# Up stage of a hybrid attention block: which k tiles take their long passes before their short ones

## The chip, the cores and the metric

The kernel runs on one core of one Trainium2 chip. The metric is the device time of one execution in microseconds (us). Three executions of the kernel before gave 1472.08, 1472.37 and 1472.39 us; the median is 1472.37 us.

## The reference, cut to what matters

One block with 256 rows of width 2048 is computed in float32: three kinds of attention with gates, an output projection, and then a feed-forward part. The change lies in the feed-forward part's first product, which the kernel calls `u`:

```python
h2 = rms_norm(x, g_ffn[l])
u = causal_depthwise_conv(h2 @ w_up[l], conv_w[l], conv_b[l])   # [256, 2048] @ [2048, 11264]
u_gate, u_val = jnp.split(u, 2, axis=-1)
x = x + (jax.nn.silu(u_gate) * u_val) @ w_down[l]
```

## The kernel before, in words

**Stages.** Memory keys and values, the input projections (tiles named `f`, `s`, `g`, `xg`), the branch products (`b`), the output projection (`xo`, `yo`), the up stage (`u`) and the down stage (`xd`, `yd`) follow each other on TensorE. The up stage is the loop at L1138.

**Two parts of every number.** A float32 value is kept as a rounded part `hi` and a remainder `lo`, and a product is made of three of the four partial products: hi by hi, hi by lo, lo by hi. For the up stage the 256 rows of the normalised input stand transposed in `hT`, one [128, 512] slice for each of 16 k tiles (a k tile is 128 of the 2048 contracted columns): its first 256 columns are the `hi` part of all rows, the other 256 the `lo` part.

**Rounds and half rounds.** The loop takes 11 values of `f0` (0, 4, ... 40; each is four blocks of 128 feed-forward columns) and for each of them two values of `s` (0 for the gate half of `w_up`, 1 for the value half). I call one pair (f0, s) a half round; there are 22, and each has 16 k tiles and four PSUM banks, one for each block of 128 columns.

**One k tile.** It has eight matmuls. A *long pass* (L1155) has a [128, 128] block of weights `hi` as the stationary operand and streams all 512 columns of `hT`. A *short pass* (L1157) has the block of weights `lo` and streams only the first 256 columns. There is one of each for each of the four banks. The list `UP_ORDER` (L39) gives them in turn: long, short, long, short and so on, bank by bank. A k tile for which `grouped` is true (L1151) is sorted by kind instead: four long passes, then four short ones. In the kernel before, the first four k tiles of each half round are grouped while f0 is 0 or 4, and only the first k tile of each half round after that.

**What feeds it.** `piece` (L136) loads two k tiles of weights (512 KB) on the SyncE queue, ScalarE rounds them to `hi` (L142) and VectorE forms `lo` (L143); `hi` and `lo` have four buffers each.

**What stands among the passes.** After each pair of k tiles `tick` lets the deferred work go on: the convolution of the half round before (`conv`, L1114), sums of weights for the down stage (`weight_sums`, L244), and in the first half round the last 16 transposes of the input (L196) after the fourth k tile. Two transposes (L1049), which spread the row scale, stand between the first and the second half round. The helper functions `in_order` and `pin` fix some of the order; the rest is put in place by a scheduler.

Of the kernel before, what the change touches and what calls it, by code (L numbers as in the profile page):

```python
# [42 lines left out]
def hybrid_block(  # L43
# [38 lines left out]
    def bank(name):  # L82
        return pp.tile([P, 512], F32, tag="bank", name=name)
# [14 lines left out]
    def later(gen):  # L98
        waiting.append(gen)
# [3 lines left out]
    def tick(beside=True):  # L103
        if beside:
            for g in background:
                next(g, None)
        while waiting and len(active) < WINDOW:
            active.append([waiting.popleft(), 0])
        for a in list(active):
            if a[1] > 0:  # L110
                a[1] -= 1
                continue
            try:
                a[1] = next(a[0]) or 0
            except StopIteration:
                active.remove(a)
# [19 lines left out]
    def piece(src, a, n, name):  # L136
        raw = wp.tile([P, PIECE], F32, tag="raw", name=f"raw_{name}")
        hi = wp.tile([P, PIECE], F32R, tag="hi", bufs=SBUFS, name=f"hi_{name}")
        lo = wp.tile([P, PIECE], F32R, tag="lo", bufs=SBUFS, name=f"lo_{name}")
        m = a * n  # L140
        pin(nc.sync.dma_start(raw[:, :m].rearrange("p (a n) -> p a n", a=a), src))
        pin(nc.scalar.copy(hi[:, :m], raw[:, :m]))  # L142
        pin(nc.vector.tensor_tensor(lo[:, :m], raw[:, :m], hi[:, :m].bitcast(F32), ALU.subtract))  # L143
        return (
            hi[:, :m].rearrange("p (a n) -> p a n", a=a),
            lo[:, :m].rearrange("p (a n) -> p a n", a=a),
        )
# [525 lines left out]
    for k in range(KT):  # L673
# [18 lines left out]
        for _ in range(0 if k < 3 else 1 if k < 8 else 3):  # L692
            if squares:
                j, t = squares.popleft()
# [419 lines left out]
    def conv(ps, f, s):  # L1114
        if not pads:
            padded()
        ct = s * FT + f
        cr = cp.tile([P, S], F32, tag="cr", bufs=2, name=f"cr_{f}_{s}")
        nc.scalar.copy(cr, ps[:, S:])
        u = pads[f % 2]  # L1120
        nc.vector.tensor_tensor(cr, cr, ps[:, :S], ALU.add)
        nc.vector.tensor_tensor(u[:, 2:], cr, rbc, ALU.mult)  # L1122
        y = cp.tile([P, S], F32, tag="y", bufs=6, name=f"y_{f}_{s}")
        tap = lambda j: taps[:, j, ct : ct + 1]
        nc.scalar.activation(y, u[:, 2:], AF.Identity, scale=tap(2), bias=tap(3))  # L1125
        nc.vector.scalar_tensor_tensor(y, u[:, 1 : S + 1], tap(1), y, ALU.mult, ALU.add)
        nc.vector.scalar_tensor_tensor(y, u[:, 0:S], tap(0), y, ALU.mult, ALU.add)
        if s == 0:
            nc.scalar.activation(y, y, AF.Silu)
            ys[f] = y  # L1130
        else:
            g = ys.pop(f)
            nc.vector.tensor_tensor(g, g, y, ALU.mult)
            split_to(a_pair(f // 2)[:, f % 2], g)
        return
        yield

    for f0 in range(0, FT, 4):  # L1138
        if f0 == FA:
            assert not halves  # L1140
            for g in background:
                deque(g, 0)
            background.clear()
        for s in range(2):
            ps = [bank(f"u{f0 + i}_{s}") for i in range(4)]
            c0 = s * D_FF + f0 * P
            for k in range(0, KT, 2):
                hi, lo = piece(upv[:, k : k + 2, c0 : c0 + 512], 2, 512, f"u{f0}_{s}_{k}")
                for j in range(2):
                    first, last = k + j == 0, k + j == KT - 1  # L1150
                    grouped = k + j < (4 if f0 < 8 else 1)  # L1151
                    for i, part in sorted(UP_ORDER, key=lambda ip: ip[1]) if grouped else UP_ORDER:
                        c = slice(i * P, (i + 1) * P)
                        if part == 0:
                            nc.tensor.matmul(ps[i], lhsT=hi[:, j, c], rhs=hT(k + j), start=first, stop=False)  # L1155
                        else:
                            nc.tensor.matmul(  # L1157
                                ps[i][:, :S], lhsT=lo[:, j, c], rhs=hT(k + j)[:, :S], start=False, stop=last
                            )
                tick()  # L1160
            for i in range(4):
                later(conv(ps[i], f0 + i, s))
# [90 lines left out]
```

## Time and profile before

| what | value |
|---|---|
| median of three executions | 1472.37 us |
| the profiled execution, its own time | 1472.16 us |
| its span in the profile | 1470.4 us |
| TensorE clock granted | 1.0 |
| first long pass of the up stage starts | 746.85 us |
| first matmul of the down stage starts | 1242.02 us |
| passes in the up stage | 1408 long, 1408 short |

The profiled execution lasted 1.8 us longer than its span, which counts from the first to the last instruction. Times in the views are counted from the span's start. A matmul's row gives its start and a duration that includes the time in the array's pipeline; consecutive matmuls overlap, so what a matmul costs is the step from its start to the start of the next.

### The profile page before, as it was taken

The numbers are of one execution on the slowest core, as the hardware profiler recorded it, in microseconds if no ns is written. First come the engines' busy times: TensorE is split into PE (matmuls) and PEld (weight loads), VectorE is DVE, ScalarE is ACT, GpSimd is POOL, SyncE is SP. The second block draws the span as 40 slices with busy tenths as digits, with TensorE's granted clock in tenths as the row PEclk, the third lists the DMA queues.
The fourth block names the chain that finished last, engine by engine and source line by source line (L and its number), as shares of the span: only waits on it lengthen the run. The fifth ranks groups of instructions, "written<-read, shape, count | busy, mean of one in ns | idle before, by whom it ended". The sixth has DMA issues, their size and how long they took to land.

```text
span 1470.4 us, 20665 instructions
## 1 busy us (share of the span) xinstructions
PE 1465.3 (100%) x7337; PEld 1239.1 (84%) x7337; DVE 1194.0 (81%) x1818; ACT 840.0 (57%) x1194; POOL 20.4 (1%) x46
## 2 busy tenths in 40 slices
PE   9999999999999999999999999999999999999998
PEld 7888888888888888888888888888888888888887
DVE  5777676777588899897888889888888877997877
ACT  6755454464364555546666556556556555674664
POOL 0000000021000000000000000000000000000000
PEclk9999999999999999999999999999999999999999
DMA  9686787687868576778768888889888866798796
GB/s 311 199 276 191 219 285 214 185 268 222 248 196 279 160 236 202 274 249 278 248 208 275 278 279 289 274 277 287 287 280 283 260 188 199 248 317 274 262 319 225
DMA packets 205527, 369.42 MB, mean 251 GB/s; under 512 B 13531, under 2 KB 82031, under 8 KB 205167
## 3 DMA queue, kind: packets, MB, share of 16 engines
q1 hardware_dynamic: 204094, 365.99, 78.0%
q10 hardware_dynamic: 1328, 2.11, 0.4%
q8 instruction: 57, 0.93, 0.2%
q14 instruction: 48, 0.39, 0.1%
HBM read 335.54 MB, written 32.51 MB: 250 GB/s over the span
## 4 chain that ended last, share of the span: by engine, by line
PE 99%; DVE 0%; ACT 0%; POOL 0%; issue 0%; POOLq 0%; DVEq 0%
PE u L1155 22%; PE u L1157 11%; PE xd L289 4%; PE xd L288 4%; PE xd L287 4%; PE xg L289 3%; PE xg L288 3%; PE xg L287 3%; PE f L289 2%; PE f L287 2%; PE f L288 2%; PE s L287 2%; PE s L289 2%; PE s L288 2%; PE b L289 2%; PE g L287 2%
## 5 line engine op out<-in xcount | busy, mean ns | idle before, releaser
L1155 PE MATMUL u<-hT,hi_u 128*128 128x512 f32 x1232 | 422.1, 395 | 0.0
L1157 PE MATMUL u<-hT,lo_u 128*128 128x256 f32 x1232 | 328.9, 280 | 0.0
L1155 PEld LDWEIGHTS u<-hT,hi_u 128*128 128x128 f32 x1232 | 228.8, 188 | 51.6
L143 DVE TENSOR_TENSOR lo_u<-raw_u,hi_u 128x1024 fp32r<-128x1024 f32 x176 | 214.9, 1221 | 68.9 <-ACT hi_u L142 67.9
L142 ACT CAST hi_u<-raw_u 128x1024 fp32r<-128x1024 f32 x176 | 184.8, 1050 | 142.9 <-PE u L1155 129.8
L1157 PEld LDWEIGHTS u<-hT,lo_u 128*128 128x128 f32 x1232 | 227.9, 189 | 2.9
L282 DVE TENSOR_TENSOR lo_d<-raw_d,hi_d 128x1024 fp32r<-128x1024 f32 x88 | 106.7, 1222 | 20.7 <-ACT hi_d L281 18.0
L281 ACT CAST hi_d<-raw_d 128x1024 fp32r<-128x1024 f32 x88 | 92.1, 1054 | 48.0 <-PE xd L288 23.0
L281 ACT CAST hi_g<-raw_g 128x1024 fp32r<-128x1024 f32 (+1 forms) x64 | 61.7, 972 | 37.2 <-PE xg L288 14.2
L282 DVE TENSOR_TENSOR lo_g<-raw_g,hi_g 128x1024 fp32r<-128x1024 f32 (+1 forms) x64 | 70.7, 1117 | 4.1 <-ACT hi_g L281 4.1
L142 ACT CAST hi_f<-raw_f 128x1024 fp32r<-128x1024 f32 (+1 forms) x40 | 38.6, 968 | 52.2 <-PE f L288 47.3
L143 DVE TENSOR_TENSOR lo_f<-raw_f,hi_f 128x1024 fp32r<-128x1024 f32 (+1 forms) x40 | 44.7, 1119 | 28.0 <-ACT hi_f L142 26.1
L288 PE MATMUL xd<-hi_d,aT 128*128 128x512 f32 x170 | 66.2, 389 | 0.0
L287 PE MATMUL xd<-hi_d,aT 128*128 128x512 f32 x170 | 66.2, 389 | 0.0
L289 PE MATMUL xd<-lo_d,aT 128*128 128x512 f32 x170 | 66.1, 389 | 0.0
L143 DVE TENSOR_TENSOR lo_s<-raw_s,hi_s 128x1024 fp32r<-128x1024 f32 (+1 forms) x40 | 44.7, 1117 | 25.3 <-ACT hi_s L142 25.0
L142 ACT CAST hi_s<-raw_s 128x1024 fp32r<-128x1024 f32 (+1 forms) x40 | 38.4, 961 | 43.9 <-PE s L288 27.1
L1155 PE MATMUL u<-hT_rest,hi_u 128*128 128x512 f32 x176 | 62.7, 396 | 0.0
L143 DVE TENSOR_TENSOR lo_g<-raw_g,hi_g 128x1024 fp32r<-128x1024 f32 x32 | 39.3, 1233 | 22.6 <-ACT hi_g L142 22.2
L1125 ACT ACTIVATE y<-u,taps 128x256 f32<-128x256 f32 x88 | 49.2, 595 | 14.5 <-DVE u L1122 14.5
L142 ACT CAST hi_b<-raw_b 128x1024 fp32r<-128x1024 f32 x32 | 33.6, 1052 | 41.6 <-PE b L288 15.3
L142 ACT CAST hi_g<-raw_g 128x1024 fp32r<-128x1024 f32 x32 | 33.6, 1051 | 37.6 <-PE g L288 35.3
(481 smaller groups left out, 3532.1 us busy)
## 6 DMA issues: line engine op xcount, KB each, us to landing
raw_u<-in_w_up_dram SPq DMA_DIRECT2D x176, 512.0 KB, 4.9
raw_g<-in_w_in_dram SPq DMA_DIRECT2D x96, 512.0 KB, 4.5
raw_d<-in_w_down_dram SPq DMA_DIRECT2D x66, 512.0 KB, 5.4
pre_d<-in_w_down_dram SPq DMA_DIRECT2D x88, 256.0 KB, 4.3
kept_d<-pre_d SPq DMA_DIRECT2D x44, 512.0 KB, 6.1
raw_f<-in_w_in_dram SPq DMA_DIRECT2D x32, 512.0 KB, 4.6
raw_s<-in_w_in_dram SPq DMA_DIRECT2D x32, 512.0 KB, 4.2
raw_o<-in_w_out_dram SPq DMA_DIRECT2D x25, 512.0 KB, 5.1
```

What stands on the lines that cost most here:

```text
L142: pin(nc.scalar.copy(hi[:, :m], raw[:, :m]))
L143: pin(nc.vector.tensor_tensor(lo[:, :m], raw[:, :m], hi[:, :m].bitcast(F32), ALU.subtract))
L281: nc.scalar.copy(hi[:, :n], src)
L282: nc.vector.tensor_tensor(lo[:, :n], src, hi[:, :n].bitcast(F32), ALU.subtract)
L287: fix(nc.tensor.matmul(o, lhsT=ah, rhs=w[0], start=first, stop=False))
L288: fix(nc.tensor.matmul(o, lhsT=al, rhs=w[0], start=False, stop=False))
L289: fix(nc.tensor.matmul(o, lhsT=ah, rhs=w[1], start=False, stop=last))
L1125: nc.scalar.activation(y, u[:, 2:], AF.Identity, scale=tap(2), bias=tap(3))
L1155: nc.tensor.matmul(ps[i], lhsT=hi[:, j, c], rhs=hT(k + j), start=first, stop=False)
L1157: nc.tensor.matmul(ps[i][:, :S], lhsT=lo[:, j, c], rhs=hT(k + j)[:, :S], start=False, stop=last)
```

## The change

One line is changed. After it, exactly one k tile of the whole stage is grouped: f0 = 4, s = 0, k tile 0, the first of the third half round. The other 33 k tiles that were grouped take long and short passes in turn.

```diff
                 for j in range(2):
                     first, last = k + j == 0, k + j == KT - 1
-                    grouped = k + j < (4 if f0 < 8 else 1)
+                    grouped = (f0, s, k + j) == (4, 0, 0)
                     for i, part in sorted(UP_ORDER, key=lambda ip: ip[1]) if grouped else UP_ORDER:
```

No pass is added or removed. The order of the built program moves on TensorE in these k tiles alone. On VectorE one `lo` (second half round, first pair of k tiles) goes ahead of the copy that feeds the two transposes of L1049. On the SyncE queue one load of the second half round's weights (k tiles 8 and 9) goes ahead of one load for the down stage. ScalarE and GpSimd keep their order.

## Prediction

> **What bounds the kernel now.** I read the page first: its span, the busy shares, the chain that ended last, and the groups of the two lines that change.
>
> ```profile
> span 1470.4 us, 20665 instructions
> ...
> PE 99%; DVE 0%; ACT 0%; POOL 0%; issue 0%; POOLq 0%; DVEq 0%
> ...
> L1155 PE MATMUL u<-hT,hi_u 128*128 128x512 f32 x1232 | 422.1, 395 | 0.0
> L1157 PE MATMUL u<-hT,lo_u 128*128 128x256 f32 x1232 | 328.9, 280 | 0.0
> ...
> L142 ACT CAST hi_u<-raw_u 128x1024 fp32r<-128x1024 f32 x176 | 184.8, 1050 | 142.9 <-PE u L1155 129.8
> ```
>
> TensorE is the chain (99%), and the passes have no idle time ahead of them (0.0 in the last column). ScalarE waits for TensorE to free weight buffers (129.8 us), not the other way round. So only the steps between matmuls can change the time. Next I asked for the stretches between the first long passes of half rounds: the first seven, then the last two.
>
> ```profile
> 746.85:770.97 24.12, 24.12 (x148) 21.36 (x146) 19.19 (x32) 17.18 (x31) 0.00 (x0) 1.00 0.68 203
> 770.97:793.62 22.65, 22.65 (x132) 19.68 (x130) 18.76 (x32) 14.21 (x21) 0.00 (x0) 1.00 0.85 267
> 793.62:816.19 22.57, 22.57 (x131) 19.62 (x129) 20.66 (x39) 13.13 (x20) 0.00 (x0) 1.00 0.86 269
> 816.19:838.76 22.57, 22.57 (x130) 19.62 (x129) 18.46 (x31) 13.18 (x20) 0.00 (x0) 1.00 0.89 291
> 838.76:860.97 22.21, 22.21 (x131) 19.57 (x130) 20.52 (x39) 13.20 (x20) 0.00 (x0) 1.00 0.86 267
> 860.97:883.57 22.60, 22.60 (x131) 19.60 (x129) 18.48 (x31) 13.10 (x20) 0.00 (x0) 1.00 0.90 294
> 883.57:905.77 22.20, 22.20 (x130) 19.56 (x129) 20.50 (x39) 13.23 (x20) 0.00 (x0) 1.00 0.85 271
> ...
> 1197.22:1219.42 22.20, 22.20 (x131) 19.56 (x129) 18.14 (x33) 13.11 (x20) 0.00 (x0) 1.00 0.62 187
> 1219.42:1242.02 22.60, 22.60 (x130) 19.60 (x129) 15.57 (x25) 13.07 (x20) 0.00 (x0) 1.00 0.61 186
> ```
>
> The first numbers are the length, then TensorE's busy time. From the fifth half round on, equal work takes 22.20 us and 22.60 us in turn, at a granted clock of 1.00. The last two rows have far less DMA (187 GB/s against 271 and 294) and the same two lengths, so transfers are not the reason. The timeline of TensorE shows it pass by pass; first from the sixth half round (22.60), then from the seventh (22.20).
>
> ```profile
> 870.14 0.40 PE L1155 MATMUL u<-hT,hi_u 128*128 128x512 f32 x1
> 870.38 0.28 PE L1157 MATMUL u<-hT,lo_u 128*128 128x256 f32 x1
> 870.50 0.40 PE L1155 MATMUL u<-hT,hi_u 128*128 128x512 f32 x1
> 870.73 0.28 PE L1157 MATMUL u<-hT,lo_u 128*128 128x256 f32 x1
> 870.85 0.40 PE L1155 MATMUL u<-hT,hi_u 128*128 128x512 f32 x1
> 871.08 0.28 PE L1157 MATMUL u<-hT,lo_u 128*128 128x256 f32 x1
> 871.20 0.40 PE L1155 MATMUL u<-hT,hi_u 128*128 128x512 f32 x1
> ```
>
> ```profile
> 889.83 0.39 PE L1155 MATMUL u<-hT,hi_u 128*128 128x512 f32 x1
> 890.05 0.28 PE L1157 MATMUL u<-hT,lo_u 128*128 128x256 f32 x1
> 890.17 0.39 PE L1155 MATMUL u<-hT,hi_u 128*128 128x512 f32 x1
> ...
> 890.52 0.39 PE L1155 MATMUL u<-hT,hi_u 128*128 128x512 f32 x1
> ```
>
> Long and short passes in turn run in one of two gaits. In the dragging gait three pairs take 1.06 us (870.14 to 871.20) and the long steps differ: 0.24, 0.23, 0.23. That is 0.3533 us a pair, 1.413 us for a k tile of four pairs. In the quick gait two pairs take 0.69 us (889.83 to 890.52). Fifteen alternating tiles of a 22.20 half round, less the grouped one worked out next, give it better: (22.20 - 1.40) / 15 = 1.387 us. A gait, once there, holds for all 15 alternating tiles. The grouped tile's own cost is in the chain that ended last, at the sixth and the seventh half round:
>
> ```profile
> 861.13 0.92 PE u L1155 x4
> 862.05 0.48 PE u L1157 x4
> 862.53 0.23 PE u L1155
> ...
> 883.73 0.93 PE u L1155 x4
> 884.66 0.47 PE u L1157 x4
> 885.13 0.23 PE u L1155
> ```
>
> 862.53 - 861.13 = 1.40 us, and 885.13 - 883.73 = 1.40 us: between the gaits. What matters is what it leaves behind. **One grouped tile turns the gait over**: quick before 861.13 and dragging after it, dragging before 883.73 and quick after it, and so on to the end. **Four in a row leave it as it was**: the second, third and fourth half rounds drag (22.65, 22.57, 22.57), though the third and fourth begin with four grouped tiles each. Check: 4 x 1.40 + 12 x 1.413 = 22.56.
>
> The TensorE page of the Trainium skill (TensorE: Matmul & The Clock Gate, "Back-to-back issue gap") gives a gap that depends on the streamed columns alone. By it the order would be worth nothing, and the time would stay 1472.4. The 22.20 and 22.60 of one workload speak against it.
>
> **The change part by part.** The profiled execution (1472.16) stands 0.2 below the median (1472.37); I sum on the first and add 0.2.
>
> The question is the gait ahead of the one tile left. The two transposes of L1049 come just before the second half round:
>
> ```profile
> 752.43 1.91 PE L196 MATMUL hT<-ident,xres_again 128*128 128x128 f32 x16
> 754.10 0.47 PE L1155 MATMUL u<-hT,hi_u 128*128 128x512 f32 x1
> 754.41 0.28 PE L1157 MATMUL u<-hT,lo_u 128*128 128x256 f32 x1
> 754.53 0.40 PE L1155 MATMUL u<-hT,hi_u 128*128 128x512 f32 x1
> ...
> 770.83 0.38 PE L1049 MATMUL rp<-ident,rb 128*128 128x128 f32 x2
> 770.97 1.18 PE L1155 MATMUL u<-hT,hi_u 128*128 128x512 f32 x4
> ```
>
> From 754.10 to 770.83 there are twelve alternating tiles: 16.73 / 12 = 1.394, quick but for the start. Then come two transposes and four grouped tiles, and the gait drags. If four grouped tiles change nothing, the two transposes did it, and without the grouped tiles the second half round drags from its start. Then the tile at (4, 0, 0) turns the gait to quick, and nothing later turns it back. I choose this. The sum:
>
> - First half round: four grouped tiles (752.43 - 746.85 = 5.58) become alternating, in a gait not seen there: 5.55 (quick) to 5.65 (dragging); I take the middle, +0.02, and keep both ends. The 16 transposes stay where they are.
> - Second: 12 tiles drag already; the first four, 22.65 - 12 x 1.413 = 5.69, become 5.65: -0.04.
> - Third: 1.40 + 15 x 1.387 = 22.20 for 22.57: -0.37.
> - Fourth: 16 x 1.387 = 22.19 for 22.57: -0.38.
> - Nine half rounds of 22.20 (s = 0) become 22.19, by unrounded steps 0.02 less: -0.16 together.
> - Nine of 22.60 (s = 1) become 22.19: 9 x -0.415 = -3.73.
>
> Together -4.66, so 1467.5, and **1467.7 us** against the median (-0.32%).
>
> Cover. A short pass is wanted earlier where grouping is gone: the first 0.23 after the start instead of 0.90. The nearest `lo` is the stage's first, and its row in VectorE's timeline is
>
> ```profile
> 742.17 1.22 DVE L143 TENSOR_TENSOR lo_u<-raw_u,hi_u 128x1024 fp32r<-128x1024 f32 x1
> ...
> 764.11 0.29 DVE L1045 COPY rb<-scales 128x256 f32<-128x256 f32 x1
> ```
>
> It ends at 743.39, 3.5 us ahead of the stage, so this costs nothing; without that cover it would be at most the 0.67 by which the use moves. The copy `rb`, now behind a `lo` of 1.22, ends near 765.6 instead of 764.40, 5 us before the transposes at 770.83 that read it. On SyncE's queue one load for the down stage comes one 512 KB load later; the down stage starts 470 us after that. Loads that start up to 2% sooner meet a DMA share of 0.85 to 0.90 with ScalarE waiting for TensorE, so nothing is late next.
>
> **The rivals.**
>
> *The transposes leave the quick gait, and the one tile turns it to dragging (slower).* For it: 16 transposes at 752.43 are followed by alternating passes directly, and these are quick from the second pair on; the two of L1049 may do the same, and the second half round's first grouped tile, which starts out of transposes, may not turn the gait as later ones do. Against it: four grouped tiles then led from quick to dragging, which four do nowhere else. It decides at the third half round's first tile. Price: second half round 22.65 to 22.20, -0.45; third 1.40 + 15 x 1.413 = 22.60, +0.03; fourth 22.61, +0.04; nine of 22.20 become 22.61, +3.67; nine of 22.60, +0.09. Sum +3.4: 1475.8 (+0.23%).
>
> *Quick everywhere.* The transposes leave the quick gait and the one tile does not turn it, because this quick gait grew out of transposes and not out of a grouped tile. The forecast less the second half round's 0.41: 1467.3.
>
> *No difference.* The gaits in the long stretches without a grouped tile fall into each other, or mix: between the two ends, 1472.4 if half of it drags as now. Against it: neither gait decays within 15 tiles anywhere.
>
> **How the numbers follow.** The forecast gets 0.52, quick everywhere 0.08, the slower rival 0.33, no difference 0.07. About 0.2% (2.9 us) is what a measurement of this kernel can tell from no change, so the slower rival (+3.4) lies just outside, and I count a small part of it as no change: faster 0.60, same 0.10, slower 0.30. The forecast's own range is 1467.0 to 1468.4 (the unknown first four tiles, the spread of runs of 0.3). It and quick everywhere hold only 0.60, so the range must reach to the slower rival: 1466.8 to 1476.2.
>
> **What would show it.** Right: the second half round takes 22.6, the third 22.2, and all later ones 22.19; the grouped tile at about 793.6 costs 1.40; the down stage starts 4.7 us sooner. Wrong: a second half round of 22.2 and 22.6 from the third on (first rival); 22.19 from the second on (quick everywhere). If the gait changes in the middle of a half round, or TensorE has idle time ahead of a pass in this stage, the whole reading is wrong.

## The result, and the profile after

| | before | after |
|---|---|---|
| median | 1472.35 us (11 runs) | 1475.68 us (11 runs) |
| profiled execution, its own time and span | 1472.16, 1470.4 us | 1475.68, 1474.0 us |
| up stage, first long pass to first matmul of the down stage | 746.85 to 1242.02: 495.17 us | 746.43 to 1245.53: 499.10 us |

The kernel after is slower: 1.0023 times the time before, 95% interval [1.0014, 1.0032]. The forecast was 1467.7 us and faster. All of the loss is in the up stage, which grew by 3.93 us; in the profiled execution the stage began 0.42 us earlier, which is why the span grew by no more than 3.6.

The profile page's group lines of the kernel after hold the first hint. They are the same two groups, long and short passes, that the prediction quotes of before: busy time, mean ns of one, idle time ahead.

```profile
L1155 PE MATMUL u<-hT,hi_u 128*128 128x512 f32 x1232 | 435.9, 399 | 0.0
L1157 PE MATMUL u<-hT,lo_u 128*128 128x256 f32 x1232 | 345.4, 281 | 0.0
```

There is no idle time ahead of a pass in either kernel, and the number of passes is the same. But a long pass lasts 399 ns in the mean and not 395, a short one 281 and not 280. The half rounds of the kernel after, the second to the fourth and the last (length first, then TensorE's busy time, granted clock as the third number from the end):

```profile
770.60:793.29 22.69, 22.69 (x131) 19.68 (x130) 18.90 (x32) 14.28 (x21) 0.00 (x0) 1.00 0.89 273
793.29:815.88 22.59, 22.59 (x130) 19.60 (x129) 20.68 (x39) 13.21 (x20) 0.00 (x0) 1.00 0.88 268
815.88:838.49 22.61, 22.61 (x130) 19.60 (x129) 18.46 (x31) 13.08 (x20) 0.00 (x0) 1.00 0.89 291
...
1222.92:1245.53 22.61, 22.61 (x131) 19.60 (x129) 15.55 (x25) 13.08 (x20) 0.00 (x0) 1.00 0.59 184
```

The second half round drags, as the forecast said. The third begins with the grouped tile, and it drags too, as does every one after it. The quick half rounds of before (22.20) are gone: nine of them lose 0.41 us each, 3.7 us; the other 13 add the remaining 0.2 or so. So the second half round came out as I had read the transposes, and **the grouped tile did not turn the gait**.

Its surroundings say why it might not. First TensorE's timeline of the kernel before, at a tile that turned the drag into the quick gait (883.57); then that of the kernel after, at its one tile (793.29).

```profile
882.86 0.40 PE L1155 MATMUL u<-hT_rest,hi_u 128*128 128x512 f32 x1
883.10 0.28 PE L1157 MATMUL u<-hT_rest,lo_u 128*128 128x256 f32 x1
883.22 0.40 PE L1155 MATMUL u<-hT_rest,hi_u 128*128 128x512 f32 x1
...
883.57 1.09 PE L1155 MATMUL u<-hT,hi_u 128*128 128x512 f32 x4
...
884.97 0.40 PE L1155 MATMUL u<-hT,hi_u 128*128 128x512 f32 x1
```

```profile
792.93 0.40 PE L1155 MATMUL u<-hT_rest,hi_u 128*128 128x512 f32 x1
793.17 0.28 PE L1157 MATMUL u<-hT_rest,lo_u 128*128 128x256 f32 x1
793.29 1.08 PE L1155 MATMUL u<-hT,hi_u 128*128 128x512 f32 x4
...
794.68 0.40 PE L1155 MATMUL u<-hT,hi_u 128*128 128x512 f32 x1
```

The dragging gait is a cycle of three pairs of a long and a short pass. The step from a long pass to the short one behind it differs between the three: to the nanosecond the trace has 241, 236 and 233 in this order (1 less in some half rounds), and I name the three places of the cycle by them. In rounded rows only the 241 stands out, as a step of 0.24. Before, it is the pair from 882.86 (883.10 - 882.86), a second pair (236) follows, and the tile stands at the third place, 233. After, the 0.24 is the last pair before the tile (793.17 - 792.93), so the tile stands at the 236 place. It is shorter as well, from its first matmul to that of the next k tile: 794.68 - 793.29 = 1.39 against 884.97 - 883.57 = 1.40.

### The profile page after: what moved, and what is told of

Its sections match the earlier page's. It is cut to its first block, busy times and chain, and to the rows that moved or that the text cites. A ratio compares the mean times of both kernels' runs of the same rounds, so it can differ in the third digit from the quotient of the medians.

```text
span 1474.0 us, 20665 instructions
## 1 busy us (share of the span) xinstructions
PE 1468.9 (100%) x7337; PEld 1239.8 (84%) x7337; DVE 1195.4 (81%) x1818; ACT 840.1 (57%) x1194; POOL 20.3 (1%) x46
## 4 chain that ended last, share of the span: by engine, by line
PE 99%; DVE 0%; ACT 0%; POOL 0%; issue 0%; POOLq 0%; DVEq 0%
PE u L1155 22%; PE u L1157 11%; PE xd L289 4%; PE xd L288 4%; PE xd L287 4%; PE xg L289 3%; PE xg L287 3%; PE xg L288 3%; PE f L289 2%; PE f L287 2%; PE f L288 2%; PE s L287 2%; PE s L289 2%; PE s L288 2%; PE g L287 2%; PE b L289 2%
## 5 line engine op out<-in xcount | busy, mean ns | idle before, releaser
L1155 PE MATMUL u<-hT,hi_u 128*128 128x512 f32 x1232 | 435.9, 399 | 0.0
L1157 PE MATMUL u<-hT,lo_u 128*128 128x256 f32 x1232 | 345.4, 281 | 0.0
L1157 PEld LDWEIGHTS u<-hT,lo_u 128*128 128x128 f32 x1232 | 232.5, 189 | 0.1
```

The source lines that it names most:

```text
L1157: nc.tensor.matmul(ps[i][:, :S], lhsT=lo[:, j, c], rhs=hT(k + j)[:, :S], start=False, stop=last)
```

## The experiments

**Theories.** *Place theory*: whether a grouped tile turns the drag depends on where in the cycle of three pairs it begins; the place 236 does not turn. *Origin theory*: a drag that grew out of the transposes cannot be turned by one tile. Smaller rivals stand with their runs. To turn means to end the drag here, and (4, 0, 1) is the k tile with f0 = 4, s = 0, k tile 1. All kernels differ from the one after in the condition of L1151 and in L1046 to L1048 alone. Times are medians; ratios are to the kernel before, run beside them.

Two things help to read them. The change had also moved a `lo` on VectorE and a load on SyncE's queue. In the traces of the kernel with no grouped tile and of all six with the tile or tiles elsewhere, VectorE, ScalarE, GpSimd and SyncE have the same order of instructions as in the kernel after, and yet some of these kernels drag and some do not; so those two moves are not the cause. And the up stage of the profiled executions began anywhere between 746.39 and 748.57 us, though the edits leave the stages ahead of it alone; differences of about 1 us between medians therefore say little, and the lengths of half rounds are the closer measure.

### No grouped tile

```diff
-                    grouped = (f0, s, k + j) == (4, 0, 0)
+                    grouped = False
```

> No k tile is grouped. Both theories: if the one grouped tile of the changed kernel did nothing but save 0.02 us, leaving it out changes nothing: 1475.7 us, the second half round and all later ones at 22.61, three pairs in 1.06 us throughout. If instead the grouped tile had kept the drag alive, the later half rounds would be 22.19 and the time about 1467.5.

Measured: 1475.64 us, ratio 1.0027 [1.0017, 1.0037]; the third half round and the last drag in its profile:

```profile
793.37:815.98 22.61, 22.61 (x131) 19.62 (x129) 20.70 (x39) 13.24 (x20) 0.00 (x0) 1.00 0.85 268
1223.02:1245.63 22.61, 22.61 (x131) 19.62 (x129) 15.54 (x25) 13.10 (x20) 0.00 (x0) 1.00 0.60 186
```

The kernel after behaves as one with no grouped tile at all, but for the 0.02 us that its tile saves in the third half round (22.59 there).

### The tile moved: five other k tiles

```diff
-                    grouped = (f0, s, k + j) == (4, 0, 0)
+                    grouped = (f0, s, k + j) == (4, 0, 1)     # and (4, 0, 2); (4, 1, 0); (0, 1, 2); (0, 1, 1)
```

The diff shows the first of five kernels; the comment gives the tiles of the other four.

> The one grouped tile is moved by one k tile, to (4, 0, 1). The dragging gait repeats every three pairs (long steps 232, 241, 236 ns) and a k tile has four, so the tile now begins one place further in the cycle, at the long pass of 232 that follows the short pass of 113, where every grouped tile of the kernel before that turned the drag began. Place theory: it turns; from there 22.19 a half round, third half round 22.23, time 1475.7 - 8.4 = 1467.2. Origin theory (a drag that grew out of the two transposes cannot be turned by one tile): no turn, 1475.7.

Measured: 1467.24 us, ratio 0.9969 [0.9957, 0.9981]. The timeline at the tile (794.73) and its half rounds:

```profile
794.02 0.40 PE L1155 MATMUL u<-hT,hi_u 128*128 128x512 f32 x1
794.26 0.28 PE L1157 MATMUL u<-hT,lo_u 128*128 128x256 f32 x1
794.38 0.40 PE L1155 MATMUL u<-hT,hi_u 128*128 128x512 f32 x1
...
794.73 1.09 PE L1155 MATMUL u<-hT,hi_u 128*128 128x512 f32 x4
...
796.13 0.40 PE L1155 MATMUL u<-hT,hi_u 128*128 128x512 f32 x1
```

```profile
793.32:815.55 22.23, 22.23 (x131) 19.57 (x129) 20.51 (x39) 13.16 (x20) 0.00 (x0) 1.00 0.83 263
815.55:837.74 22.19, 22.19 (x131) 19.57 (x130) 18.41 (x31) 13.06 (x20) 0.00 (x0) 1.00 0.92 303
1214.91:1237.10 22.19, 22.19 (x131) 19.57 (x130) 15.52 (x25) 13.01 (x20) 0.00 (x0) 1.00 0.61 190
```

The 0.24 pair (794.02), one more pair, then the tile: the place of the kernel before. It turns, and the quick gait holds for the 19 half rounds that follow. The origin theory falls with this run: this drag grew out of the same transposes.

> The one grouped tile at (4, 0, 2), where the cycle stands at its 241 ns long pass. No grouped tile seen so far began there. Place theory in its narrow form (only the place after the 113 ns short pass turns): no turn, 1475.7. Place theory with two good places: 1467.3. Origin theory: 1475.7.

Measured: 1467.67 us, ratio 0.9971 [0.9959, 0.9982]. It turns too. In its timeline the 0.24 pair (795.54) is the third last before the tile at 796.60, so the tile stands where the next 241 was due:

```profile
795.54 0.40 PE L1155 MATMUL u<-hT,hi_u 128*128 128x512 f32 x1
795.78 0.28 PE L1157 MATMUL u<-hT,lo_u 128*128 128x256 f32 x1
795.90 0.40 PE L1155 MATMUL u<-hT,hi_u 128*128 128x512 f32 x1
...
796.25 0.40 PE L1155 MATMUL u<-hT,hi_u 128*128 128x512 f32 x1
...
796.60 1.11 PE L1155 MATMUL u<-hT,hi_u 128*128 128x512 f32 x4
...
798.01 0.40 PE L1155 MATMUL u<-hT,hi_u 128*128 128x512 f32 x1
```

So the narrow form (the 233 place alone turns) was wrong: two of three places turn, the 241 place on the evidence of this one kernel. The tile costs 798.01 - 796.60 = 1.41 here.

> The one grouped tile at (4, 1, 0): again the first k tile of a half round and of a load, as in the changed kernel, but 64 pairs later, which is one place further in the cycle of three (64 = 21 x 3 + 1), the same place as (4, 0, 1). Place theory: it turns, fourth half round 22.20, later ones 22.19, time 1475.7 - 8.0 = 1467.7. If what matters is that the tile is the second one of a load (another reading of a turn at (4, 0, 1)): no turn, 1475.7. Origin theory: no turn, 1475.7.

Measured: 1468.70 us, ratio 0.9978 [0.9967, 0.9988]. The third, fourth and fifth half rounds:

```profile
793.26:815.87 22.61, 22.61 (x131) 19.62 (x129) 20.70 (x39) 13.22 (x20) 0.00 (x0) 1.00 0.87 273
815.87:838.07 22.20, 22.20 (x130) 19.56 (x129) 18.39 (x31) 13.07 (x20) 0.00 (x0) 1.00 0.90 291
838.07:860.26 22.19, 22.19 (x131) 19.57 (x130) 20.53 (x39) 13.22 (x20) 0.00 (x0) 1.00 0.86 272
```

The turn comes with the tile, at the first k tile of a load; so a turn does not need the second k tile of a load, as at (4, 0, 1). The median is 1.0 above the expectation, while the profiled execution, 1467.60, agrees with it.

> The one grouped tile as early as it can stand at the 233 ns place: in the profile of the kernel without grouped tiles the first three tiles of the second half round begin after the transposes, at the 236 place, and at the 233 place. So the tile is (0, 1, 2). Place theory: it turns; second half round 1.49 + 1.41 + 1.40 + 13 x 1.387 = 22.33, all later ones 22.19, time 1475.6 - 8.9 = 1466.8, the lowest so far. Rival (a turn needs a whole half round of settled drag ahead of it, as the turns at (4, 0, 1), (4, 0, 2) and (4, 1, 0) had): no turn, 1475.6.

Measured: 1467.87 us, ratio 0.9973 [0.9962, 0.9983]; second half round 22.33 and later ones 22.19, as expected:

```profile
771.24:793.57 22.33, 22.33 (x131) 19.65 (x130) 18.74 (x32) 14.29 (x21) 0.00 (x0) 1.00 0.86 270
793.57:815.76 22.19, 22.19 (x131) 19.57 (x130) 20.53 (x39) 13.21 (x20) 0.00 (x0) 1.00 0.88 273
```

The 0.24 pair begins at 773.43 and is the second last ahead of the tile at 774.14, as at (4, 0, 1). The gaits came out to the hundredth; the median is 1.1 above the sum and so not told apart from the other kernels that turn.

> The one grouped tile one k tile earlier than in the run beside it, at the 236 ns place where the changed kernel's tile stood. Place theory: no turn, steps of the tile near 227, 227, 226 ns after the first long pass, the second half round 22.69 less 0.02, later ones 22.61, time 1475.6. Rival (the changed kernel's tile failed for another reason that belongs to (4, 0, 0), such as the bank that conv still reads): this one turns, 1466.8.

Measured: 1476.49 us, ratio 1.0029 [1.0018, 1.0040]. The second and third half rounds:

```profile
771.59:794.26 22.67, 22.67 (x131) 19.69 (x130) 18.76 (x32) 14.22 (x21) 0.00 (x0) 1.00 0.85 270
794.26:816.87 22.61, 22.61 (x130) 19.60 (x129) 20.70 (x39) 13.21 (x20) 0.00 (x0) 1.00 0.86 269
```

In its timeline the 0.24 pair (772.72 to 772.96) is the last ahead of the tile at 773.08. No turn at the 236 place, in another half round than the changed kernel's. The median is 0.9 above the expectation; the half rounds are as expected. One k tile between this run and the last decides over 0.5%.

### Two grouped tiles

```diff
-                    grouped = (f0, s, k + j) == (4, 0, 0)
+                    grouped = (f0, s) == (4, 0) and k + j < 2
```

> Two grouped tiles, (4, 0, 0) and (4, 0, 1). The rule of my forecast (an even number of grouped tiles leaves the gait as it was): drag to the end, 1475.6. Place theory: the first tile leaves the drag, as it did alone, and ends on short steps of 120 ns with a long pass of 233 next; the second then begins at the 233 place and turns: later half rounds 22.19, time 1467.2.

Measured: 1468.26 us, ratio 0.9973 [0.9963, 0.9984]. The timeline of the two tiles (795.31 and 796.70) and the third and fourth half rounds:

```profile
794.95 0.40 PE L1155 MATMUL u<-hT_rest,hi_u 128*128 128x512 f32 x1
795.19 0.28 PE L1157 MATMUL u<-hT_rest,lo_u 128*128 128x256 f32 x1
795.31 1.08 PE L1155 MATMUL u<-hT,hi_u 128*128 128x512 f32 x4
...
796.70 1.09 PE L1155 MATMUL u<-hT,hi_u 128*128 128x512 f32 x4
```

```profile
795.31:817.52 22.21, 22.21 (x131) 19.57 (x130) 20.51 (x39) 13.13 (x20) 0.00 (x0) 1.00 0.86 273
817.52:839.70 22.18, 22.18 (x130) 19.56 (x129) 18.40 (x31) 13.05 (x20) 0.00 (x0) 1.00 0.91 297
```

The first tile stands right after the 0.24 pair (794.95), the place that does not turn, and takes 1.39 as in the changed kernel. The second begins at the 233 place and turns. An even number of tiles did not leave the gait as it was, so the counting rule of the forecast is wrong, not only unlucky. The median is 1.1 above the expectation; the half rounds are as expected.

### The transposes

The forecast's other step was that the two transposes leave the drag. In the first kernel they wait for three calls of `tick` and not for four.

```diff
-            yield 4
+            yield 3
```

(without a grouped tile)

> No grouped tile, and the two transposes of L1049 issued one call of tick sooner, ahead of k tile 14 of the first half round and not at the border of the half rounds. If the two transposes end the quick gait: k tiles 14 and 15 of the first half round already drag (1.41) and so does all that follows, 1475.7. If the border of the half rounds ends it (new banks, a new round of loads): quick to the border, then drag, 1475.6, with the change seen at the border. If neither, but the exact place of the transposes among the passes: the gait after them can be quick, and then the time is near 1466.7.

Measured: 1475.83 us, ratio 1.0028 [1.0017, 1.0038]. The transposes at their new place, ahead of k tile 14:

```profile
767.76 0.38 PE L1049 MATMUL rp<-ident,rb 128*128 128x128 f32 x2
767.90 0.48 PE L1155 MATMUL u<-hT_rest,hi_u 128*128 128x512 f32 x1
768.21 0.28 PE L1157 MATMUL u<-hT_rest,lo_u 128*128 128x256 f32 x1
768.33 0.40 PE L1155 MATMUL u<-hT_rest,hi_u 128*128 128x512 f32 x1
...
769.39 0.40 PE L1155 MATMUL u<-hT_rest,hi_u 128*128 128x512 f32 x1
```

768.33 to 769.39 are three pairs in 1.06 us: the drag begins with the transposes, inside the half round. It does not need the border.

```diff
-            for t in range(NT):
+            for t in 2 * list(range(NT)):       # 8 * in the other kernel
                 nc.tensor.transpose(rp[:, t * P : (t + 1) * P], rb[:, t], ident)
```

(without a grouped tile; the further transposes write the same values again)

> No grouped tile; the two transposes of L1049 are done twice, four in a row at the border of the first two half rounds (the second pair writes the same values again). Each adds a step of 0.11 us. If any row of transposes that interrupts the quick gait leaves the drag: second half round 22.9, later ones 22.61, time 1475.9. If their number decides: quick is possible, later half rounds 22.19, time near 1466.9. If four act as two pairs that each turn the gait over: quick as well.

Measured in one run: 1467.00 us beside 1471.78 for the kernel before. Four transposes leave the quick gait; the second and third half rounds:

```profile
770.89:793.16 22.27, 22.27 (x132) 19.49 (x130) 18.68 (x31) 13.79 (x21) 0.00 (x0) 1.00 0.88 273
793.16:815.34 22.18, 22.18 (x130) 19.39 (x129) 20.52 (x39) 13.20 (x20) 0.00 (x0) 1.00 0.86 266
```

> No grouped tile; the pair of L1049 is done eight times, sixteen in a row as in the first half round, after which the passes ran quick. Adds 14 x 0.109 = 1.5 us. If a long row wipes out what came before and leaves quick: later half rounds 22.19, time about 1475.6 - 8.9 + 1.5 = 1468.2. If what decides is the gait that came before (drag turns to quick at the sixteen, quick to drag at the two): drag, 1477.2.

Measured in one run: 1479.22 us beside 1471.78. Sixteen leave the drag, which speaks against a long row wiping the past out:

```profile
772.49 1.91 PE L1049 MATMUL rp<-ident,rb 128*128 128x128 f32 x16
774.16 0.48 PE L1155 MATMUL u<-hT,hi_u 128*128 128x512 f32 x1
...
774.94 0.40 PE L1155 MATMUL u<-hT,hi_u 128*128 128x512 f32 x1
...
776.00 0.40 PE L1155 MATMUL u<-hT,hi_u 128*128 128x512 f32 x1
```

Again three pairs from 774.94 to 776.00 take 1.06. That the gait ahead alone decides does not hold either, since four transposes stood behind the same quick gait and left it quick. Of the 1479.22, 2.0 us are not in the sum of 1477.2; the up stage of this execution began at 748.46, 2.0 later than that of the kernel after, so they lie in earlier stages.

> The kernel with four transposes and no grouped tile again, now timed. Its one look showed 22.19 us in all half rounds after the second and 1467.0 us. If the place at which the drag begins is a matter of the order of instructions alone: the same gaits again and 1467.0 to 1467.9. If chance of the single execution had a part in it: drag in some executions, times up to 1475.8.

Measured: 1467.45 us, ratio 0.9968 [0.9957, 0.9980], with the same gaits in its profile. Without any grouped tile it is faster than the kernel before, and its interval lies wholly below that of the kernel after. It overlaps with those of all kernels whose tile turns, so these are not ranked.

> Four transposes, and the one grouped tile at (4, 0, 0) as in the changed kernel; it now stands in a quick gait that grew out of transposes (long steps of 231 and 233 ns in turn, a gait in which no grouped tile has stood so far). The slower rival of my forecast: it turns the quick gait to drag, 22.61 from the third half round on, 1475.6 - 0.1. The rival of quick everywhere: it does not turn, 22.19 or so throughout, 1467.2.

Measured: 1475.72 us, ratio 1.0026 [1.0016, 1.0036]. The profiled execution was the longest of the nine, 1477.60. Its second and third half rounds:

```profile
772.96:795.23 22.27, 22.27 (x132) 19.48 (x130) 18.68 (x31) 13.81 (x21) 0.00 (x0) 1.00 0.88 273
795.23:817.81 22.58, 22.58 (x130) 19.60 (x129) 20.67 (x39) 13.23 (x20) 0.00 (x0) 1.00 0.84 267
```

The same tile (4, 0, 0) that could not end the drag ends the quick gait, although this quick gait grew out of transposes. The other engines have the same order here as in the kernel with four transposes and no grouped tile, so the tile alone makes the difference.

## Why the prediction was wrong, point by point

- **What bounds the kernel: right.** TensorE's steps alone moved the time, no pass waits in either kernel, and two gaits of 22.19 and 22.61 a half round make up all of the difference.
- **"The two transposes did it": right.** The second half round is 22.69, and moving the transposes moved the start of the drag. That a row of transposes leaves the drag is no rule: four left the quick gait.
- **"Four in a row leave it as it was": right for the kernel before, wrong as a rule.** Two tiles at (4, 0) did not leave it. In the kernel before, the third and fourth half rounds' first tiles stood at the 233 place, and their four tiles have, alternately, the steps of a tile that turns the drag (long steps near 233, 236, 228 and 233 ns) and of one that turns it back (235, 233, 236 and 224). That four leave the gait because each turns it is read from these steps; no run tests it alone.
- **"Then the tile at (4, 0, 0) turns the gait to quick": this step failed.** I had seen single tiles turn the drag nine times and read it as what a tile does. All nine stood at one place of the cycle, 233: between eight of them and the grouped tile ahead lay 15 alternating tiles, 60 pairs, and between the first of the nine and the one ahead 12 tiles, 48 pairs; both are multiples of three. With the grouped tiles gone, the tile came 64 pairs after the transposes and stood at the 236 place, the one of three that does not turn: it cost 1.39 us and left the drag, 22.59 in its half round and 22.61 or 22.62 in the 19 after it. One k tile later the tile turns and the time is 1467.24; one half round later it turns too, with a median of 1468.70 (profiled execution 1467.60). The forecast was 1467.7.
- **The sum.** Two terms were small misses: the second half round was 22.61 in the forecast, which left out the slow start after the transposes, and is 22.69; the first was to grow by 0.02 and grew by 0.05 (24.12 before, 24.17 after), because its first four tiles drag (5.65 us, the upper end of the forecast). The third half round was 22.20 in the forecast and the 19 after it 22.19; they are 22.59 and 22.61 to 22.62. These 20 make up all but 0.1 of the 8.6 us by which the stage is longer than forecast.
- **The slower rival** gave 1475.8, and 1475.68 was measured, but by another way: it had the second half round quick and the tile turning it to drag. That the two numbers meet is luck: the 20 half rounds from the third on drag in both. With four transposes that mechanism does occur. What happened here, a drag from the second half round on that the tile does not turn, was none of the rivals, although "quick everywhere" had the same doubt about a quick gait that grew out of transposes.
- **The range** reached to the slower rival and held the time by that luck; the direction was wrong.
- **The Trainium skill's rule.** A gap set by the streamed columns alone (the Trainium skill, TensorE: Matmul & The Clock Gate, "Back-to-back issue gap") would make the kernels with equal passes equal. The section gives this formula for an isolated matmul, which the prediction left out; for a stream of weight loads and matmuls it says that both set the spacing, and it has no price for the order of the passes. Equal numbers of passes took 1467.24 and 1475.64 us here.

## What to carry to other kernels

When a regular stream of unequal matmuls runs in one of two gaits, look at the steps between starts and not at durations, which barely show it (399 against 395 ns in the mean), or idle time, which is none in both; then find the length of the gait's cycle and where in it the disturbance falls (here three pairs, while a k tile has four). Nine equal observations that lie a multiple of the cycle apart are one observation. A version that depends on this should be looked at in the profile after every edit ahead of it, since two more transposes or one k tile moved the time by 0.5%.

## What the runs showed of the hardware that I had not expected

- Long and short passes in turn keep their gait through the whole stage: 20 half rounds, 1280 pairs, with no change in either direction (dragging in the kernel after, quick with the tile at (0, 1, 2)), through changes of buffers, banks and DMA load (184 to 303 GB/s in the half rounds shown).
- A grouped tile in a drag takes 1.39 at the place that does not turn and 1.40 or 1.41 at those that do.
- At the border of the first two half rounds, where they interrupt the quick gait, two transposes leave the drag, four the quick gait and sixteen the drag (the sixteen in one execution). The sixteen in the first half round left the quick gait, also in the kernel without grouped tiles, where they interrupt a drag (the k tiles ahead of them took 1.40 to 1.42 us). What sets the gait inside TensorE is not settled by these runs, and neither is why the 236 place does not turn. What they show is that the gait goes with the order of the matmuls ahead: it differs between kernels whose other engines have the same order, and came out the same in both profiles of the kernel with four transposes.
